# Block 1 of a three-block layer: convolution sums moved from SBUF to PSUM, compressed-attention operands split once

## The chip, the cores and the metric

The kernel runs on one core of a Trainium2 chip. The metric is the device time of one execution in microseconds (us). Five engines work side by side, each through its own queue in program order: TensorE (PE in the profile, its weight loads PEld), VectorE (DVE), ScalarE (ACT), GpSimd (POOL) and SyncE (SP), which here issues the DMAs. SBUF is the on-chip working memory; PSUM has 8 banks of 128 x 512 fp32, and PE writes its products there.

## The reference, cut to what matters

Three blocks follow each other over 512 tokens of 1024 features. The change lies in the first, which sums an attention branch with three parts and a convolution branch:

```python
def compress_blocks(t, pos_emb, w1, w2):            # 31 blocks of 32 tokens, for each of 4 groups
    ...
    return jax.nn.silu(blocks @ w1) @ w2

# in nsa_attention, for every block of 128 queries:
s_c = jnp.einsum('bgrqd,bgnd->bgrqn', qb, k_c).astype(jnp.float32) * scale
p_c = masked_softmax(s_c, c_end[None, :] <= tpos[:, None])
o_c = jnp.einsum('bgrqn,bgnd->bgrqd', p_c.astype(dt), v_c)
...
return gb[..., 0:1] * o_c + gb[..., 1:2] * o_s + gb[..., 2:3] * o_w

# in conformer_conv: 31 taps over time, each feature for itself, then a layer norm
z = u_a * jax.nn.sigmoid(u_b)
zp = jnp.pad(z, ((0, 0), (CONV_WIDTH - 1, 0), (0, 0)))
z = lax.conv_general_dilated(zp, conv_w, window_strides=(1,), padding='VALID', ...) + conv_b
```

With 512 tokens all 8 selection blocks are taken (top 16 of 8), so the selected branch `o_s` is a causal attention over all keys, like the window branch `o_w`.

## The kernel before

Features lie on partitions, tokens along the free axis; a matrix of 1024 features is eight tiles of 128x512. Nearly every product is made of three fp32r products: each operand is split into a high part and the rest (`h`, `l`), and `gemm` (L169 to L177) issues `h*h`, `l*h`, `h*l` for each of 8 steps, so 24 matmuls of 512 columns into one PSUM bank. Weights come by DMA into `wst` and are split by ACT (`wh`, L158) and POOL (`wl`, L159).

Block 1 up to the norm behind the convolution is one stage in which everything runs at once:

- **Convolution** (`conv_gate`, `conv_in`, `conv_taps`, L652 to L682). For each of eight feature tiles `c` two products give `z`, 128 x (30 + 512) in SBUF. `conv_taps` starts the sum `y = X[:, c]` with tap 0 on ACT (L672), then 30 taps on DVE (L682), each reading `z` shifted, the tap's weight (one per partition) and `y`, and writing `y`. All taps have low priority (`LOW` = 3000), so they stand where DVE would otherwise have nothing to do. `X` holds eight tiles, so several sums can be open at once.
- **Compressed branch.** `compress` makes the 31 compressed keys and values of four groups, `done_k` and `done_v` leave them in `kcT` and `vcs` (fp32). For each group `compressed(g, qs)` (L875 to L922) splits its keys into two zero-padded operands `KCz` with 16 small ACT and DVE instructions (L880 to L883), makes the scores, the softmax and the transposed probabilities `pcT`, and splits the values (L917 to L921). `mix_compressed` (L966 to L972) splits the probabilities of 128 queries, one head at a time, into two zero-padded operands `PCz` (ACT L969, DVE L970) and multiplies them, as the first products of the output bank `O`.
- **Selected and window branches.** `scores` (L924) and `mix` (L953) for each group `g`, 4 query blocks and 2 branches: scores to PSUM, maximum on DVE (L938), exponential on ACT (L939), scaling on ACT or POOL, transposes on PE (L957), split by ACT (L960) and DVE (L961), products (L963, L964).
- Between them stand projections and gates by a list of letters (`ORD`).

The order of instructions on each engine comes from a scheduler that lays them out ahead of the run by its own costs and the priorities; on the chip each engine takes its queue in that order.

PSUM in this stage: three banks for products (`g`), two for scores, two for transposes, one for `O`:

```python
K.psum(g=3, s=2, pt=2, o=1)
...
y = X[:, c]
nc.scalar.activation(y, z[:, 0:T], AF.Identity, scale=w(0), bias=K.v("conv_b", c))
for k in range(30, n, -1):          # n is 0 here
    nc.vector.scalar_tensor_tensor(y, z[:, k:k + T], w(k), y, op0=MUL, op1=ADD)
...
for h in range(4):                  # mix_compressed
    r = slice(h * 32, (h + 1) * 32)
    nc.scalar.activation(PCz[0][r, h], pcT[r, i * P:(i + 1) * P], AF.Copy)
    nc.vector.tensor_tensor(PCz[1][r, h], pcT[r, i * P:(i + 1) * P], PCz[0][r, h], SUB)
```

Behind the stage the `Norm` (L250 on) subtracts a shift from each tile of `X` (L309), sums the tiles and their squares (L280), takes column sums on PE (L201), makes mean and inverse deviation (L324 to L227), and the normed tiles become the operands `zn` of the next product with `w_conv_out`. Beside this PE makes eight more projections (`sgc`, evicted by L688).

Of the kernel before, what the change touches and what calls it, by code (L numbers as in the profile page):

```python
# [19 lines left out]
P = 128  # L20
# [26 lines left out]
TAP = ""  # L47
TC0, TC1 = 4,8
TPB = 1
# [20 lines left out]
class Ker:  # L70
# [133 lines left out]
    def rstd(self, ps, scale, eps, out, sl=slice(0, T), back=True):  # L204
        """(scale * ps + eps)^-1/2: from the logarithm, and a step of Newton's."""
# [8 lines left out]
    def newton(self, v, out, t, meanwhile=None, back=True):  # L214
        """out <- v^-1/2; v and t are lost."""
# [34 lines left out]
class Norm:  # L250
    """Layer norm over the eight [P, T] tiles of X, in place, without gain and bias.

    A tile is fed as soon as it is there. The mean of the first two shifts all of them, so that one
    pass gives the variance. With a gain and a bias [P, 8], the first products behind the norm start
    ahead of its statistics, on the shifted tiles times the gain: r * (product - mu * W'gain) + W'bias."""
# [26 lines left out]
    def square(self, k, s):  # L282
        """s: squares that belong to the variance."""
# [57 lines left out]
    def head(self, units):  # L341
        """Products of the first units (weights, outputs each) with the norm's result, all but the last steps of each."""
# [37 lines left out]
class Vecs:  # L380
    """Per-feature vectors, one column for 128 features each."""
# [28 lines left out]
def _pos_cols(a):  # L410
    # [32, 64] -> [128 = (copy, d), e * 16 + kt] of value a[2 kt + e, d]
# [25 lines left out]
def _dm(w):  # L437
    """[K, M] -> [M/128, 128, K]: the stationary tiles of one block of 128 outputs side by side."""
# [5 lines left out]
def _group(a, n):  # L444
    """[U, 128, C] -> [U/n, 128, n*C]: n units side by side."""
# [4 lines left out]
def _dmk(w, cuts):  # L450
    """As _dm, with K cut in parts: part after part, flat."""
# [8 lines left out]
def _tm(w, per):  # L460
    """[K, M] -> [K/128/per, 128, per*M]: moving tiles, per k tiles in a unit."""
# [132 lines left out]
def block1(K, X, entry):  # L594
    """X: the residual tile [P, 8, T]; takes the input from DRAM, leaves the output before the last norm."""
# [3 lines left out]
    K.psum(g=3, s=2, pt=2, o=1)  # L599
# [7 lines left out]
    # operands g * x and the rms of x, applied behind the products  # L607
# [60 lines left out]
    def conv_taps(c, z):  # L668
        y = X[:, c]
        w = lambda k: K.v("conv_w", c * 31 + k)  # L670
        with tc.high_priority(offset=-LOW):
            nc.scalar.activation(y, z[:, 0:T], AF.Identity, scale=w(0), bias=K.v("conv_b", c))  # L672
            n = len(TAP) if TC0 <= c < TC1 else 0
            for k in range(n):
                t = pz.tile([P, T], F32, tag="tb", bufs=TPB, name=K.nm("tb"))
                if TAP[k] == "A":
                    nc.scalar.activation(t, z[:, k + 1:k + 1 + T], AF.Copy, scale=w(k + 1))
                else:
                    nc.gpsimd.tensor_tensor(t, z[:, k + 1:k + 1 + T], w(k + 1).to_broadcast([P, T]), MUL)
                nc.gpsimd.tensor_tensor(y, y, t, ADD)  # L680
# [22 lines left out]
    def roped(w, scale=1.0, out=None):  # L703
        """A projection times the rms factor, rotated: its sine and cosine have the factor."""
# [15 lines left out]
    def gates():  # L720
        # gates of the three branches, tokens on partitions
# [12 lines left out]
    # compressed keys and values  # L734
    def compress(pB, kv, src, done):
        """src: two [P, T] tiles of (group, d) rows; by quarters; done gets the transposed hidden layer and w2."""
# [37 lines left out]
        hT = pB.tile([P, 256], F32, tag="hT", name=K.nm("hT"))  # L774
        nc.vector.tensor_scalar(hT, pt[:, :256], 0.5, None, op0=MUL)
        w2 = pB.tile([P, 128], F32, tag="w2", name=K.nm("w2"))
        nc.sync.dma_start(w2, I[f"cw2_{kv}"][0])
# [46 lines left out]
    # static zero-padded operands of the compressed branch  # L824
    KCz = []
    PCz = []
    for i in range(2):
        t = pA.tile([P, 4, P], F32R, name=f"KCz{i}")
        nc.gpsimd.memset(t.bitcast(F32), 0.0)
        KCz.append(t)  # L830
        t = pA.tile([P, 4, P], F32R, name=f"PCz{i}")
# [3 lines left out]
    def values(pair):  # L835
        """Values of two groups, tokens on partitions: [tok, j, branch, (h | l)] each."""
# [38 lines left out]
    def compressed(g, qs):  # L875
        """Scores of the four heads over the compressed keys, softmax, transposed back: probabilities and values."""
        src = kcT[:, g * 32:(g + 1) * 32]
        for h in range(4):
            c = slice(h * 32, (h + 1) * 32)
            nc.scalar.activation(KCz[0][0:64, h, c], src, AF.Copy)  # L880
            nc.scalar.activation(KCz[0][64:128, h, c], src, AF.Copy)
            nc.vector.tensor_tensor(KCz[1][0:64, h, c], src, KCz[0][0:64, h, c], SUB)
            nc.vector.tensor_tensor(KCz[1][64:128, h, c], src, KCz[0][0:64, h, c], SUB)  # L883
        ps = K.ps("pt")
        for h in range(4):
            for e in range(2):
                nc.tensor.matmul(ps, lhsT=KCz[e][:, h], rhs=qs[h], start=h == 0 and e == 0, stop=h == 3 and e == 1)
        sT = pT.tile([P, T], F32, tag="ct", bufs=2, name=K.nm("ct"))
# [4 lines left out]
        sc = pT.tile([P, T], F32, tag="ct", bufs=2, name=K.nm("ct"))  # L893
# [1193 lines left out]
```

## Time and profile before

| | |
|---|---|
| Median of three runs | 2956.25 us (2956.14 to 2957.11) |
| Span of the profiled execution | 2957.2 us |
| First tap starts, last tap starts (of the 240) | 77.4 us, 583.7 us |
| First product of `w_conv_out` starts | 620.8 us |
| Busy over the whole span | PE 91%, DVE 62%, POOL 45%, ACT 44% |

No other time is given for the profiled execution than its span, which is 0.95 us above the median. "Busy" counts the time in which an engine has an instruction in work; for PE the ends are modelled, so a busy PE need not run at its peak. Mean durations are those of one instruction; where the next one of an in-order engine overlaps its end, the next one starts earlier than the duration says. PEclk is the granted share of TensorE's clock. A stretch is a piece of the span between two times; here the stretches are cut at the first tap (77.4), at the four times when a group's compressed scores reach DVE (222.3, 307.8, 393.9, 476.8), at the last tap (583.7) and at the first product behind the norm (620.8).

### The profile page before, as it was taken

To read this page: it belongs to the slowest core of one execution; us is meant where nothing else is said; L and a number is where in the kernel's file an instruction comes from. 1 tells how busy PE (TensorE), PEld (TensorE's weight loads), DVE (VectorE), ACT (ScalarE), POOL (GpSimd) and SP (SyncE) were. 2 spreads that over 40 slices of the span, in tenths; PEclk is the share of its full clock that TensorE was granted. 3 is DMA by queue.
4 is the path that set the end of the run, shared out by engine and by line. 5 is a ranking of instruction groups with operands and counts; after the bars stand their busy time and mean duration, and the time that the engine had idled before them with its cause. 6 is when DMAs were issued, how large, how long until landed. Compare 5 with 4: busy or idle time off the path is not lost.

```text
span 2957.2 us, 34250 instructions
## 1 busy us (share of the span) xinstructions
PE 2701.9 (91%) x12194; PEld 2137.6 (72%) x12194; DVE 1847.5 (62%) x2893; ACT 1295.3 (44%) x2396; POOL 1336.8 (45%) x1023
## 2 busy tenths in 40 slices
PE   7778998899999998888889999999989889999997
PEld 5556766677888875666667778887766668788885
DVE  7999999986342477676675831115877865422246
ACT  3337786443222254354344433332556652322233
POOL 6564343444444454333332544444555334444442
PEclk9889999999999999999999999999999899999998
DMA  3221111132232322322321222223232122222223
GB/s 113 93 80 45 45 39 50 51 107 93 93 100 93 100 73 79 87 65 62 90 65 59 79 90 96 94 97 110 82 104 72 50 72 93 93 93 94 99 93 100
DMA packets 78666, 243.26 MB, mean 82 GB/s; under 512 B 10528, under 2 KB 14793, under 8 KB 78497
## 3 DMA queue, kind: packets, MB, share of 16 engines
q1 hardware_dynamic: 78496, 241.09, 25.3%
q8 instruction: 96, 1.57, 0.2%
q14 instruction: 74, 0.60, 0.1%
HBM read 230.90 MB, written 4.52 MB: 80 GB/s over the span
## 4 chain that ended last, share of the span: by engine, by line
PE 59%; DVE 22%; ACT 5%; DMA 3%; issue 2%; POOL 1%; DVEq 0%; ACTq 0%; SPq 0%; POOLq 0%
PE pg L174 17%; PE pg L175 17%; PE pg L176 17%; DVE X L682 2%; DMA B<-diag 2%; DVE p L1896 1%; DVE QK L1312 1%; DMA diag<-dg 1%; DVE X L339 1%; PE ppt L957 1%; DVE PTl L961 1%; DVE ln L280 1%; PE ps L935 1%; DVE s L938 1%; DVE Zt L1418 1%
## 5 line engine op out<-in xcount | busy, mean ns | idle before, releaser
L159 POOL TENSOR_TENSOR wl<-wst,wh 128x512 fp32r<-128x512 f32 (+1 forms) x808 | 1111.2, 1381 | 1347.5 <-ACT wh L158 1260.3
L158 ACT ACTIVATE wh<-wst 128x512 fp32r<-128x512 f32 (+1 forms) x808 | 500.3, 627 | 1106.8 <-PE pg L175 918.5
L174 PE MATMUL pg<-op,wh 128*128 128x512 f32 (+1 forms) x2008 | 813.2, 405 | 12.8 <-ACT wh L158 6.7
L176 PE MATMUL pg<-op,wl 128*128 128x512 f32 (+1 forms) x2008 | 809.9, 403 | 10.0 <-POOL wl L159 10.0
L175 PE MATMUL pg<-op,wh 128*128 128x512 f32 (+1 forms) x2008 | 807.2, 402 | 1.4 <-DVE op L194 1.4
L174 PEld LDWEIGHTS pg<-op,wh 128*128 128x128 f32 (+1 forms) x2008 | 387.5, 193 | 92.9 <-ACT wh L158 7.3
L176 PEld LDWEIGHTS pg<-op,wl 128*128 128x128 f32 (+1 forms) x2008 | 387.0, 193 | 91.9 <-POOL wl L159 13.5
L175 PEld LDWEIGHTS pg<-op,wh 128*128 128x128 f32 (+1 forms) x2008 | 387.3, 193 | 80.7 <-DVE op L194 3.9
L174 PE MATMUL pg<-hid,wh 128*128 128x512 f32 x688 | 272.2, 396 | 0.8 <-DVE hid L193 0.8
L175 PE MATMUL pg<-hid,wh 128*128 128x512 f32 x688 | 271.8, 395 | 1.3 <-DVE hid L194 1.3
L176 PE MATMUL pg<-hid,wl 128*128 128x512 f32 x688 | 272.1, 396 | 0.0
L682 DVE SCALAR_TENSOR_TENSOR X<-z,vec,X 128x512 f32<-128x512 f32 x240 | 233.6, 1006 | 1.3
L1122 DVE TENSOR_TENSOR X<-X,pg 128x512 f32<-128x512 f32 x56 | 38.6, 689 | 222.4 <-PE pg L176 222.4
L175 PEld LDWEIGHTS pg<-hid,wh 128*128 128x128 f32 x688 | 129.2, 188 | 33.0 <-DVE hid L194 1.6
L174 PEld LDWEIGHTS pg<-hid,wh 128*128 128x128 f32 x688 | 129.2, 188 | 32.8 <-DVE hid L193 1.3
L176 PEld LDWEIGHTS pg<-hid,wl 128*128 128x128 f32 x688 | 129.2, 188 | 31.5 <-issue 0.2
L193 DVE CAST hid<-t 128x512 fp32r<-128x512 f32 x86 | 52.2, 607 | 147.1 <-ACT t L1099 146.3
L939 ACT ACTIVATE P<-ps,s 128x128 f32<-128x128 f32 (+3 forms) x128 | 66.3, 522 | 20.6 <-DVE s L938 17.3
L1113 DVE SCALAR_TENSOR_TENSOR t<-pg,R 128x512 f32<-128x512 f32 x32 | 22.1, 692 | 84.0 <-PE pg L176 83.9
L194 DVE TENSOR_TENSOR hid<-t,hid 128x512 fp32r<-128x512 f32 x86 | 64.7, 752 | 3.0
L938 DVE TENSOR_REDUCE s<-ps 128x1 f32<-128x128 f32 (+3 forms) x128 | 59.4, 481 | 7.7 <-PE ps L937 6.7
L935 PE MATMUL ps<-sk,sk 128*128 128x256 f32 (+2 forms) x128 | 48.8, 382 | 8.2 <-ACT P L939 7.6
(524 smaller groups left out, 4445.8 us busy)
## 6 DMA issues: line engine op xcount, KB each, us to landing
wst<-in_w_f_dram SPq DMA_DIRECT2D x64, 512.0 KB
wst<-in_w_up_dram SPq DMA_DIRECT2D x32, 512.0 KB
wst<-in_w_down_dram SPq DMA_DIRECT2D x32, 512.0 KB
wst<-in_w_ga_dram SPq DMA_DIRECT2D x24, 512.0 KB
wst<-in_w_fg_dram SPq DMA_DIRECT2D x22, 512.0 KB
wst<-in_w_fu_dram SPq DMA_DIRECT2D x22, 512.0 KB
wst<-in_w_q_dram SPq DMA_DIRECT2D x16, 512.0 KB
wst<-in_w_out_dram SPq DMA_DIRECT2D x16, 512.0 KB
```

Source lines behind the costliest of these rows:

```text
L158: nc.scalar.activation(h, st, AF.Copy)
L159: nc.gpsimd.tensor_tensor(l, st, h, SUB)
L174: self.nc.tensor.matmul(ps, lhsT=wh, rhs=h[:, sl], start=first and k == 0, stop=False)
L175: self.nc.tensor.matmul(ps, lhsT=wh, rhs=l[:, sl], start=False, stop=False)
L176: self.nc.tensor.matmul(ps, lhsT=wl, rhs=h[:, sl], start=False, stop=last and k == n - 1)
L193: nc.vector.tensor_copy(h, src)
L194: nc.vector.tensor_tensor(l, src, h, SUB)
L682: nc.vector.scalar_tensor_tensor(y, z[:, k:k + T], w(k), y, op0=MUL, op1=ADD)
L935: nc.tensor.matmul(S[:, :N], lhsT=ql, rhs=kh[:, :N], start=True, stop=False)
L938: nc.vector.tensor_reduce(mx[:, h:h + 1], S[:, :L], AX, MAX, negate=True)
L939: nc.scalar.activation(Pt[h][:, :L], S[:, :L], AF.Exp, bias=mx[:, h:h + 1], accum_out=den[:, h:h + 1])
L1122: nc.vector.tensor_tensor(X[:, m], X[:, m], ps, ADD)
```

## The change

Five things change, all in block 1:

1. The sum of a convolution tile is held in a PSUM bank `y`, of which there is one; ACT starts it there with tap 0, DVE adds 30 taps in place, and ACT copies the end to `X[:, c]`. One product bank is given up for it (`g=2`).
2. `done_k` splits the compressed keys of all groups at once (`KC`), on 128 partitions; for each group two ACT copies with a broadcast put four heads of them into `KCz`, which is 640 wide, so that one instruction reaches all four diagonal blocks.
3. `done_v` splits the values of all groups at once (`VC`, four copies of a group's 32 rows by a wider `hT`).
4. The transposed probabilities are split straight from PSUM into `PCz`, for two query blocks at a time (`pad_compressed`): 8 ACT and 8 DVE instructions a group where there were 16 and 16.
5. The compressed products are the last of an output bank instead of the first.

Dead code of the taps goes (`TAP` is the empty string), and comments; the lines are renumbered by two or three.

```diff
-    K.psum(g=3, s=2, pt=2, o=1)
+    K.psum(g=2, s=2, pt=2, o=1, y=1)
...
-    kcT = pA.tile([64, P], F32, name="kcT")
-    vcs = pA.tile([P, 64], F32, name="vcs")
+    KC = [pA.tile([P, P], F32R, name=f"KC{e}") for e in range(2)]
+    VC = pA.tile([P, 4, P], F32R, name="VC")
...
     def conv_taps(c, z):
-        y = X[:, c]
         w = lambda k: K.v("conv_w", c * 31 + k)
         with tc.high_priority(offset=-LOW):
+            y = K.ps("y")
             nc.scalar.activation(y, z[:, 0:T], AF.Identity, scale=w(0), bias=K.v("conv_b", c))
...
-            for k in range(30, n, -1):
+            for k in range(30, 0, -1):
                 nc.vector.scalar_tensor_tensor(y, z[:, k:k + T], w(k), y, op0=MUL, op1=ADD)
+            nc.scalar.activation(X[:, c], y, AF.Copy)
...
-        hT = pB.tile([P, 256], F32, tag="hT", name=K.nm("hT"))
-        nc.vector.tensor_scalar(hT, pt[:, :256], 0.5, None, op0=MUL)
...
+        n = 1 if kv == "k" else 4
+        hT = pB.tile([P, 8, n, 32], F32, tag=f"hT{kv}", name=K.nm("hT"))
+        nc.vector.tensor_scalar(hT, pt[:, :256].rearrange("p (a n) -> p a n", n=32)[:, :, None, :].to_broadcast([P, 8, n, 32]), 0.5, None, op0=MUL)
...
+        nc.scalar.activation(KC[0], ps[:, :P], AF.Copy)
+        nc.vector.tensor_tensor(KC[1], ps[:, :P], KC[0], SUB)
...
+        nc.scalar.activation(VC[:, :, 0:64], src, AF.Copy)
+        nc.vector.tensor_tensor(VC[:, :, 64:128], src, VC[:, :, 0:64], SUB)
...
     def compressed(g, qs):
-        src = kcT[:, g * 32:(g + 1) * 32]
-        for h in range(4):
-            c = slice(h * 32, (h + 1) * 32)
-            nc.scalar.activation(KCz[0][0:64, h, c], src, AF.Copy)
-            nc.scalar.activation(KCz[0][64:128, h, c], src, AF.Copy)
-            nc.vector.tensor_tensor(KCz[1][0:64, h, c], src, KCz[0][0:64, h, c], SUB)
-            nc.vector.tensor_tensor(KCz[1][64:128, h, c], src, KCz[0][0:64, h, c], SUB)
+        for e in range(2):
+            src = KC[e][:, g * 32:(g + 1) * 32][:, None, :].to_broadcast([P, 4, 32])
+            nc.scalar.activation(KCz[e].rearrange("p (h c) -> p h c", h=4)[:, :, 0:32], src, AF.Copy)
...
+        return sc
+
+    def pad_compressed(sc, half):
         ps = K.ps("pt")
-        for i in range(4):
-            nc.tensor.transpose(ps[:, i * P:(i + 1) * P], sc[:, i * P:(i + 1) * P], K.ident)
-        pcT = pT.tile([P, T], F32, tag="pcT", bufs=1, name=K.nm("pcT"))
-        nc.scalar.activation(pcT, ps, AF.Copy)
...
+        for a in range(2):
+            i = 2 * half + a
+            nc.tensor.transpose(ps[:, a * P:(a + 1) * P], sc[:, i * P:(i + 1) * P], K.ident)
         for h in range(4):
-            nc.scalar.activation(VC[h * 32:(h + 1) * 32, 64:128], vl[gs], AF.Copy)
-        return pcT, VC
+            r = slice(h * 32, (h + 1) * 32)
+            src = ps[r, :256].rearrange("p (a q) -> p a q", a=2)
+            nc.scalar.activation(PCz[0][r, :, h], src, AF.Copy)
+            nc.vector.tensor_tensor(PCz[1][r, :, h], src, PCz[0][r, :, h], SUB)
...
-                mix_compressed(O, i, pcT, VC)
-            mix(O, g, i, b, Pt, VS[g // 2][g % 2], False, b == 1)
+            mix(O, g, i, b, Pt, VS[g // 2][g % 2], b == 0, False)
             if b == 1:
+                mix_compressed(O, g, i)
+                if i == 1:
+                    pad_compressed(sc, 1)
```

Beside the code, the order on the engines moves. Three places matter. The first is VectorE in the first stretch. Names ending in a number are buffers: `z_472` and `z_581` are the inputs of the tiles 0 and 1 of the convolution, `X` holds all sums. Before:

```order
L682 SCALAR_TENSOR_TENSOR X<-z_472,vec,X 128x512
L682 SCALAR_TENSOR_TENSOR X<-z_581,vec,X 128x512
L655 TENSOR_TENSOR zb_739<-pg_704,R_43_242 128x512
L682 SCALAR_TENSOR_TENSOR X<-z_472,vec,X 128x512
L682 SCALAR_TENSOR_TENSOR X<-z_581,vec,X 128x512
```

The same place in the change, where `z_473` and `z_584` are the inputs of tiles 0 and 1, and `py_476` is the bank with the sum of tile 0:

```order
L673 SCALAR_TENSOR_TENSOR py_476<-z_473,vec,py_476 128x512 x6
L660 SCALAR_TENSOR_TENSOR t_582<-pg_547,R_43_242 128x512
L673 SCALAR_TENSOR_TENSOR py_476<-z_473,vec,py_476 128x512
L663 SCALAR_TENSOR_TENSOR z_584<-zb_544,t_582 128x512
L673 SCALAR_TENSOR_TENSOR py_476<-z_473,vec,py_476 128x512 x11
L653 TENSOR_TENSOR zb_744<-pg_709,R_43_242 128x512
L673 SCALAR_TENSOR_TENSOR py_476<-z_473,vec,py_476 128x512 x4
```

Before, taps of two sums stood in turn. Now one sum runs at a time: 130 of the 240 taps stand directly behind a tap of their own sum, where 23 did.

The second place is VectorE at the end of the convolution. Before (`X<-X,c` shifts a tile for the norm, `ln` are its sums, `mu` its mean):

```order
L682 SCALAR_TENSOR_TENSOR X<-z_4682,vec,X 128x512 x4
L688 TENSOR_TENSOR t_5549<-pg_5514,R_43_242 128x512
L682 SCALAR_TENSOR_TENSOR X<-z_4682,vec,X 128x512 x6
L688 TENSOR_TENSOR t_5588<-pg_5553,R_43_242 128x512
L682 SCALAR_TENSOR_TENSOR X<-z_4682,vec,X 128x512 x2
L309 TENSOR_TENSOR X<-X,c_5368 128x512
L280 TENSOR_TENSOR ln_5364<-ln_5364,X 128x512
L280 TENSOR_TENSOR ln_5372<-ln_5372,ln_5404 128x512
L324 TENSOR_SCALAR mu_5412<-pm_5408 128x512
```

In the change, from the end of tile 6 (`py_3670`) and all of tile 7 (`py_4552`) on:

```order
L673 SCALAR_TENSOR_TENSOR py_3670<-z_3667,vec,py_3670 128x512 x4
L673 SCALAR_TENSOR_TENSOR py_4552<-z_4549,vec,py_4552 128x512 x30
L296 SCALAR_TENSOR_TENSOR ln_5222<-c_5226,ln_5222 128x512
L306 TENSOR_TENSOR X<-X,c_5226 128x512 x4
L277 TENSOR_TENSOR ln_5230<-ln_5230,ln_5233 128x512
L277 TENSOR_TENSOR ln_5222<-ln_5222,X 128x512
```

The 30 taps of the last tile now stand in one block behind the attention's last instructions, and all of the norm's shifts and sums behind them. Between the last tap and `mu` stood 3 instructions and stand 23.

The third place is ScalarE in the norm, from the square of the mean to the inverse deviation (`r`), with the loads of its tables of functions (`gc` is the hyperbolic tangent of a projection, `ln` and `r` logarithm and exponential). Before:

```order
L326 ACTIVATE ln_5415<-mu_5412 128x512
L212 ACT_TABLE_LOAD
L158 ACTIVATE wh_5677<-wst_5671 128x512
L219 ACTIVATE ln_5415<-ln_5417 128x512
L220 ACTIVATE r_5413<-ln_5415 128x512
L212 ACT_TABLE_LOAD
```

In the change:

```order
L323 ACTIVATE ln_5273<-mu_5270 128x512
L209 ACT_TABLE_LOAD
L1015 ACT_TABLE_LOAD
L1015 ACTIVATE gc_5332<-t_5368 128x512
L216 ACT_TABLE_LOAD
L216 ACTIVATE ln_5273<-ln_5275 128x512
L155 ACTIVATE wh_5453<-wst_5451 128x512
L217 ACT_TABLE_LOAD
L217 ACTIVATE r_5271<-ln_5273 128x512
```

A tangent with its table now stands inside, and the program has three table loads more (77, and 74 before). From within the products with `w_conv_out` on, all engines have their instructions in the same order as before.

## Rows read from the trace of the kernel before

**Rows 1.** Page, busy tenths of PE and DVE in 40 slices of the span

```profile
PE   7778998899999998888889999999989889999997
DVE  7999999986342477676675831115877865422246
```

**Rows 2.** Windows by stretch: time, busy PE, PEld, DVE, ACT, POOL (instructions), PEclk, DMA

```profile
77.40:222.30 144.90, 108.50 (x493) 85.94 (x493) 135.85 (x166) 46.65 (x100) 90.52 (x55) 0.83 0.27 86
222.30:307.80 85.50, 75.98 (x388) 57.28 (x387) 79.20 (x160) 68.11 (x185) 36.11 (x30) 0.96 0.11 37
307.80:393.90 86.10, 77.72 (x435) 61.02 (x434) 81.64 (x159) 62.17 (x161) 36.49 (x31) 0.98 0.15 46
393.90:476.80 82.90, 74.68 (x375) 55.73 (x374) 80.02 (x147) 61.44 (x154) 35.64 (x29) 0.98 0.17 51
476.80:583.70 106.90, 96.38 (x473) 73.52 (x472) 103.56 (x177) 65.60 (x160) 38.71 (x28) 0.99 0.15 52
583.70:620.80 37.10, 30.22 (x99) 20.33 (x99) 35.39 (x43) 22.04 (x35) 19.64 (x13) 0.78 0.26 86
750.00:800.00 50.00, 50.00 (x219) 40.88 (x218) 17.34 (x23) 13.05 (x23) 23.46 (x21) 1.00 0.28 85
```

**Rows 3.** Groups by form, DVE, 0 to 660 us: count, busy us, mean ns, idle

```profile
L682 DVE SCALAR_TENSOR_TENSOR X<-z,vec,X 128x512 f32<-128x512 f32 x240 | 233.6, 1006 | 1.3
L961 DVE TENSOR_TENSOR PTl<-ppt,PTh 128x512 fp32r<-128x512 f32 x80 | 52.8, 682 | 3.0 <-ACT PTh L960 2.5
L970 DVE TENSOR_TENSOR PCz<-pcT,PCz 32x128 fp32r<-32x128 f32 x64 | 27.7, 432 | 1.1
...
L688 DVE TENSOR_TENSOR t<-pg,R 128x512 f32<-128x512 f32 x16 | 10.9, 680 | 0.0
...
L883 DVE TENSOR_TENSOR KCz<-kcT,KCz 64x32 fp32r<-64x32 f32 x16 | 6.3, 393 | 0.3
...
L882 DVE TENSOR_TENSOR KCz<-kcT,KCz 64x32 fp32r<-64x32 f32 x16 | 5.1, 318 | 0.2
...
L770 DVE SCALAR_TENSOR_TENSOR t<-t,pg 128x256 f32<-128x256 f32 x2 | 0.8, 406 | 0.0
```

**Rows 4.** The tile X on DVE: shortest, median, longest of one tap in ns

```profile
L682 DVE SCALAR_TENSOR_TENSOR X<-z,vec,X x240: 714/746/1878, 77.4 to 583.7; 128x512 f32<-128x512 f32 x120
```

**Rows 5.** Timelines of DVE and of POOL at 547 us: start, us

```profile
546.70 2.45 DVE L682 SCALAR_TENSOR_TENSOR X<-z,vec,X 128x512 f32<-128x512 f32 x2
...
547.05 1.54 POOL L159 TENSOR_TENSOR wl<-wst,wh 128x512 fp32r<-128x512 f32 x1 [6.38 <-ACT wh L158]
```

**Rows 6.** Timeline of DVE: two taps of different sums, merged

```profile
113.12 1.40 DVE L682 SCALAR_TENSOR_TENSOR X<-z,vec,X 128x512 f32<-128x512 f32 x2
```

**Rows 7.** Chain that ended last: start, us, two taps of one sum

```profile
580.05 0.76 DVE X L682
580.84 0.76 DVE X L682
```

**Rows 8.** Groups, PE, 222.3 to 476.8 us: count, busy us, mean ns, idle and releaser

```profile
L174 PE MATMUL pg<-op,wh 128*128 128x512 f32 x126 | 53.7, 426 | 0.0
...
L957 PE MATMUL ppt<-ident,P 128*128 128x128 f32 x240 | 40.8, 287 | 2.4 <-POOL P L950 2.1
L964 PE MATMUL po<-PTl,VS 128*128 128x512 f32 x60 | 26.2, 436 | 11.3 <-DVE PTl L961 11.3
```

**Rows 9.** Groups, ACT, 0 to 660 us: count, busy us, mean ns, idle

```profile
L672 ACT ACTIVATE X<-z,vec 128x512 f32<-128x512 f32 x8 | 6.5, 812 | 33.3 <-DVE z L665 33.3
...
L212 ACT ACT_TABLE_LOAD x4 | 5.1, 1283 | 0.1
...
L913 ACT ACTIVATE pcT<-ppt 128x512 f32<-128x512 f32 x4 | 2.4, 595 | 9.5 <-PE ppt L911 9.5
```

**Rows 10.** Chain that ended last, from the norm's mean on: start, us

```profile
585.93 2.09 PE pm L201 x2
...
620.78 1.22 PE pg L174 x2
```

More of the change, by code (lines that the diff above doesn't have):

```diff
@@ L46 @@
 GA = 2
-TAP = ""
-TC0, TC1 = 4,8
-TPB = 1
 EV = (4,4,5)
@@ L668, in conv_taps @@
     def conv_taps(c, z):
-        y = X[:, c]
         w = lambda k: K.v("conv_w", c * 31 + k)
         with tc.high_priority(offset=-LOW):
+            y = K.ps("y")
             nc.scalar.activation(y, z[:, 0:T], AF.Identity, scale=w(0), bias=K.v("conv_b", c))
[L673 to L680, printed above, removed]
-            for k in range(30, n, -1):
+            for k in range(30, 0, -1):
                 nc.vector.scalar_tensor_tensor(y, z[:, k:k + T], w(k), y, op0=MUL, op1=ADD)
+            nc.scalar.activation(X[:, c], y, AF.Copy)
     def proj(w, scale=None, out=None):
@@ L773, in compress @@
             nc.tensor.transpose(pt[:, j * P:(j + 1) * P], hsl[:, j * P:(j + 1) * P], K.ident)
-        hT = pB.tile([P, 256], F32, tag="hT", name=K.nm("hT"))
-        nc.vector.tensor_scalar(hT, pt[:, :256], 0.5, None, op0=MUL)
-        w2 = pB.tile([P, 128], F32, tag="w2", name=K.nm("w2"))
-        nc.sync.dma_start(w2, I[f"cw2_{kv}"][0])
+        n = 1 if kv == "k" else 4
+        hT = pB.tile([P, 8, n, 32], F32, tag=f"hT{kv}", name=K.nm("hT"))
+        nc.vector.tensor_scalar(hT, pt[:, :256].rearrange("p (a n) -> p a n", n=32)[:, :, None, :].to_broadcast([P, 8, n, 32]), 0.5, None, op0=MUL)
+        hT = hT.rearrange("p a h n -> p (a h n)")
+        w2 = pB.tile([P, 2, 2, 64], F32, tag="w2", name=K.nm("w2"))
+        for e in range(2 if kv == "k" else 1):
+            nc.sync.dma_start(w2[:, :, e], I[f"cw2_{kv}"][0].rearrange("p (j d) -> p j d", j=2))
         done(hT, w2)
@@ L783, in done_k @@
         for j in range(2):
-            nc.tensor.matmul(ps[:64, :P], lhsT=w2[:, j * 64:(j + 1) * 64], rhs=hT[:, j * P:(j + 1) * P], start=j == 0, stop=j == 1)
-        nc.vector.tensor_copy(kcT, ps[:64, :P])
+            nc.tensor.matmul(ps[:, :P], lhsT=w2[:, j].rearrange("p c d -> p (c d)"), rhs=hT[:, j * P:(j + 1) * P], start=j == 0, stop=j == 1)
+        nc.scalar.activation(KC[0], ps[:, :P], AF.Copy)
+        nc.vector.tensor_tensor(KC[1], ps[:, :P], KC[0], SUB)
     def done_v(hT, w2):
         ps = K.ps("pt")
-        for j in range(2):
-            nc.tensor.matmul(ps[:, :64], lhsT=hT[:, j * P:(j + 1) * P], rhs=w2[:, j * 64:(j + 1) * 64], start=j == 0, stop=j == 1)
-        nc.vector.tensor_copy(vcs, ps[:, :64])
+        for g in range(4):
+            for j in range(2):
+                h = hT[:, (4 * j + g) * P:(4 * j + g + 1) * P]
+                nc.tensor.matmul(ps[:, g * 64:(g + 1) * 64], lhsT=h, rhs=w2[:, j, 0], start=j == 0, stop=j == 1)
+        src = ps[:, :256].rearrange("p (g d) -> p g d", g=4)
+        nc.scalar.activation(VC[:, :, 0:64], src, AF.Copy)
+        nc.vector.tensor_tensor(VC[:, :, 64:128], src, VC[:, :, 0:64], SUB)
     def seq(fs):
@@ L825, in block1 @@
     KCz = []
+    for i in range(2):
+        t = pA.tile([P, 640], F32R, name=f"KCz{i}")
+        nc.gpsimd.memset(t.bitcast(F32), 0.0)
+        KCz.append(t)
     PCz = []
     for i in range(2):
[L828 to L831, printed above, removed]
+        t = pA.tile([P, 2, 4, P], F32R, name=f"PCz{i}")
         nc.gpsimd.memset(t.bitcast(F32), 0.0)
@@ L886, in compressed @@
             for e in range(2):
-                nc.tensor.matmul(ps, lhsT=KCz[e][:, h], rhs=qs[h], start=h == 0 and e == 0, stop=h == 3 and e == 1)
-        sT = pT.tile([P, T], F32, tag="ct", bufs=2, name=K.nm("ct"))
+                nc.tensor.matmul(ps, lhsT=KCz[e][:, h * P:(h + 1) * P], rhs=qs[h], start=h == 0 and e == 0, stop=h == 3 and e == 1)
+        sT = K.tmp()
         nc.scalar.activation(sT, ps, AF.Copy)
@@ L892, in compressed @@
             nc.tensor.transpose(ps[:, i * P:(i + 1) * P], sT[:, i * P:(i + 1) * P], K.ident)
-        sc = pT.tile([P, T], F32, tag="ct", bufs=2, name=K.nm("ct"))
+        sc = pT.tile([P, T], F32, tag="ct", bufs=1, name=K.nm("ct"))
         four = lambda t: t.rearrange("p (i h n) -> p i h n", i=4, h=4)
@@ L964, in mix, with mix_compressed @@
             nc.tensor.matmul(O, lhsT=V, rhs=tl, start=False, stop=last and j == i)
-    def mix_compressed(O, i, pcT, VC):
-        for h in range(4):
-            r = slice(h * 32, (h + 1) * 32)
-            nc.scalar.activation(PCz[0][r, h], pcT[r, i * P:(i + 1) * P], AF.Copy)
-            nc.vector.tensor_tensor(PCz[1][r, h], pcT[r, i * P:(i + 1) * P], PCz[0][r, h], SUB)
+    def mix_compressed(O, g, i):
         for e in range(2):
-            nc.tensor.matmul(O, lhsT=VC, rhs=PCz[e].rearrange("p h q -> p (h q)"), start=e == 0, stop=False)
+            nc.tensor.matmul(O, lhsT=VC[:, g], rhs=PCz[e][:, i % 2].rearrange("p h q -> p (h q)"), start=False, stop=e == 1)
     todo["q"] = seq([f for g in range(4) for f in keys_queries(g)])
@@ L981, in block1 @@
         fill = list(ORD[2 + g])
-        pcT, VC = compressed(g, qs)
+        sc = compressed(g, qs)
+        pad_compressed(sc, 0)
         steps = [(i, b) for i in range(4) for b in range(2)]
```

6 lines of the change are left out of this document (removed).

## The prediction, made before the changed kernel was run

> **What bounds the kernel now.** I read the page's slices first. PE is at seven to nine tenths in every slice and DVE at nine only in the first seven and a half, some 560 us [rows 1]. So I cut that piece into stretches [rows 2]. From the first tap to the last (506.3 us) DVE is busy for 135.9 + 79.2 + 81.6 + 80.0 + 103.6 = 480.3 us, 95%, while PE loses time: its idle time before the products with the split probabilities ends on DVE, 11.3 us in three stretches [rows 8]. DVE sets the end of this piece. Behind it comes the norm, 37.1 us from the last tap to the next product at 620.8 us [rows 2, 10]; behind that, PE bounds the rest and the order does not change, so what is won or lost by 620.8 us goes into the total one for one.
>
> Where does DVE's time go? The taps are nearly half of it: 233.6 us for 240 [rows 3]. Their mean is 1006 ns, but their median only 746 and their longest 1878 [rows 4]. The timelines show what makes the slow ones: two taps took 2.45 us while POOL was in a weight split of 1.54 us [rows 5]. Both read two tensors from SBUF. The instructions of the same width with one input in PSUM do not show it: 680 and 682 ns on average over 16 and 80 [rows 3].
>
> **The change part by part, as VectorE's work.**
>
> *The slow taps.* With the sum in PSUM, a tap reads one tensor from SBUF. I take it to run like the undisturbed ones now, 746 ns: 240 x (1006 - 746) = -62.4 us [rows 3, 4]. No row has DVE writing to PSUM, so the price of that is unknown. From below it is bounded by the 680 ns of an instruction that reads PSUM without a weight per partition, another -16 us; from above by the 1006 ns of now, which would take back all 62. I stay at 746, since the nearest rows show no difference between reading PSUM (682) and SBUF.
>
> [...]
>
> *One sum at a time.* Two taps of different sums took 1.40 us, so the second started 0.66 us after the first [rows 6]; two of one sum start 0.79 us apart [rows 7]. Of the taps 130 now stand behind their own sum instead of 23, 107 x 0.12 = +12.8 us.
>
> *Operands of the compressed branch.* The probabilities cost 64 x 432 ns = 27.7 us; now 32 instructions of 256 elements with an input in PSUM, 406 ns by the nearest row, 13.0 us: -14.7. The keys' 6.3 + 5.1 us become one instruction of 128x128 (under 0.41): -11.0 [rows 3]. The values' few small ones and the wider `hT` I set at nothing together; each is below 1.5 us, and either sign lies inside the rounding.
>
> Sum for DVE: -62.4 + 12.8 - 14.7 - 11.0 = -75.3 us.
>
> *What ACT gets.* Fewer and larger instructions, eight copies of 0.60 us more [rows 9]. It is busy for 61 to 68 us of the 83 to 86 in a group's stretch [rows 2], so this costs nothing as long as no one waits for a particular one. Someone does at each change of tile: the bank is free when ACT has copied it (0.60) and begun the next sum (0.81) [rows 9], some 1.5 us with the handing over. By the new order four of the seven changes have five or more other instructions of DVE between the sums, three have none or one: 3 x 1.5 = +4.5 us. From below nothing, if the tap behind is not late; from above 7 x 1.5.
>
> *The norm.* It still begins in order behind the last taps, but with 20 more instructions between the last tap and the mean. They are moved, not added, and stand in DVE's sum already. New in series are ACT's copy and the shift it makes behind it, 2 x 0.6, a first square of 0.6, and three table loads of 1.28 [rows 9]: +5.7, say 6. PE makes more of its eight projections behind the mean instead of under the taps: 135 matmuls of 0.228 us (50 us over 219, [rows 2]) are 31 us, and the mean to the next product took 35 us before (585.9 to 620.8, [rows 10]). [...]
>
> *What is late next: PE.* In the three middle stretches (254.5 us) I count PE's matmuls in the program by their columns, 0.228 us for 512: 378 of projections (126 groups of three, [rows 8]), 216 others of 512, 48 of 384, 193 of 256, 264 transposes of 128 columns (240 of them in [rows 8]) and 96 small ones, about 196 us. DVE has 240.9 there now; of the 75 some 45 fall here, so 196 too. Two engines that hand work to each other in a fixed order cannot both be full. DVE now idles 13.6 us of these 254.5 [rows 2]; I take 31, so that both are at 86%: +18 us. From below 0; from above 35, the products' share of time in which PE stands now.
>
> **Total:** -75.3 + 4.5 + 6 + 18 = -47 us. The profiled span is 2957.2 us, so 2910; against the median, 0.95 lower, 2956.25 - 47 = 2909.
>
> **The rivals.**
>
> *Everything full.* The waits do not grow (0 for 18, 1 for 4.5) and the taps take nearer 700 ns (-8): -76, 2880 us. For it: DVE was 97% busy beside PE at 90% in the fourth and fifth stretch. Against: PE has as much to do as DVE there now.
>
> *Two banks are too few.* The compress products hold one bank over other projections in the first stretch, and DVE's order there has up to 11 taps in a row (11 x 0.79 = 8.7 us) between two evictions, when a projection lasts 24 x 0.228 = 5.5 us. Then PE waits up to 3 us at some ten projections and comes late to everything: +25, 2934 us. Against: PE stood idle there anyway, 36 of 145 us [rows 2].
>
> *Nothing gained in the taps.* The weight per partition comes from SBUF as well; if POOL's splits held the tap up by that, 1006 ns would stay: -47 + 62 = +15, 2971 us. Against: it would be a second reader of one word only.
>
> *One bank, read and written by the same instruction.* The slower side, one mechanism at one place: no row has an engine reading and writing the same PSUM bank element by element. If the two passes took turns, a tap would cost one more pass of 512, twice what 256 more elements cost (680 - 406 = 274 ns), 0.55 us: 240 x 0.55 = 132, total +85, 3041 us. It decides from a tap of 746 + 47000/240 = 942 ns on. Against it: PE adds to a bank at 0.228 us for 512 columns, a read and a write each.
>
> **How the numbers follow.** The forecast (-30 to -63) has 0.48, everything full 0.20, two banks too few (-6 to -30) 0.16, nothing gained in the taps 0.05, the bank read and written in turn 0.05; 0.06 is for a result within 0.2% (5.9 us, about what a measurement can tell from no change). So faster 0.84, same 0.06, slower 0.10. The range from 2872 (the full case with taps somewhat cheaper yet) to 2944 leaves out the last part of the two-bank case, the same and the slower ones, about 0.18, and little below.
>
> **What would show it.** Right: taps in `py` at 700 to 800 ns with no long ones; DVE's busy share in the middle stretches near 86%, these 76 us long each; the last tap near 515 us, the first product of `w_conv_out` 57 to 60 us behind it; the rest of the span as before. Wrong: taps above 940 ns; a middle stretch still at 83 us with DVE below 80%, its idle time ended by PE or by ACT's copies; PE idle before projections with their releaser in DVE's evictions.

## The result

The changed kernel takes 2909.84 us, the median of four runs (2904.16 to 2911.59), beside 2956.68 for the kernel before (2956.14 to 2957.11): a ratio of 0.9843, with a 95% interval of 0.9828 to 0.9859. That is 46.8 us less; 47 were forecast. Measured again later it was 2906.5 us and 0.9825 (0.981 to 0.9839).

The windows of the changed kernel, cut at the events of [rows 2] as far as the last tap (first tap, a group's compressed scores four times, last tap), with a last one up to where the last operand of the norm is ready; then its DVE groups for 0 to 660 us and the taps as a tile. The columns are those of before.

```profile
77.40:185.90 108.50, 96.30 (x511) 78.73 (x512) 94.58 (x139) 42.76 (x79) 66.79 (x54) 0.98 0.32 103
185.90:261.70 75.80, 74.44 (x398) 56.55 (x397) 69.79 (x139) 62.49 (x162) 34.27 (x32) 1.00 0.18 59
261.70:339.00 77.30, 73.87 (x432) 58.78 (x432) 69.57 (x143) 59.06 (x147) 32.97 (x30) 1.00 0.17 51
339.00:415.20 76.20, 72.08 (x371) 54.42 (x370) 68.38 (x129) 58.19 (x137) 33.67 (x30) 1.00 0.18 54
415.20:518.00 102.80, 85.47 (x414) 63.20 (x412) 93.70 (x168) 56.61 (x139) 21.06 (x20) 0.92 0.10 35
518.00:578.00 60.00, 45.47 (x166) 34.29 (x167) 56.16 (x72) 36.73 (x57) 35.27 (x19) 0.79 0.28 86
```

```profile
L673 DVE SCALAR_TENSOR_TENSOR py<-z,vec,py 128x512 f32<-128x512 f32 x240 | 180.2, 751 | 10.9 <-ACT py L671 6.2
...
L921 DVE TENSOR_TENSOR PCz<-ppt,PCz 32x256 fp32r<-32x256 f32 x32 | 13.4, 419 | 2.2 <-ACT PCz L920 1.3
...
L941 DVE TENSOR_TENSOR s<-s,GT 128x4 f32<-128x4 f32 x32 | 11.4, 356 | 0.1
...
L663 DVE SCALAR_TENSOR_TENSOR z<-zb,t 128x512 f32<-128x512 f32 x8 | 9.8, 1220 | 0.0
...
L336 DVE TENSOR_TENSOR X<-X,r 128x512 f32<-128x512 f32 x8 | 9.4, 1220 | 0.0
...
L194 DVE SCALAR_TENSOR_TENSOR zn<-X,zn 128x512 fp32r<-128x512 f32 x8 | 7.5, 939 | 0.0
```

```profile
L673 DVE SCALAR_TENSOR_TENSOR py<-z,vec,py x240: 718/756/757, 77.4 to 518.0; 128x512 f32<-128x512 f32 x120
```

Read the last row against [rows 4]: no tap takes longer than 757 ns, where the longest took 1878. The last tap starts at 518.0 instead of 583.7 us. The stretches went from 144.9, 85.5, 86.1, 82.9 and 106.9 us [rows 2] to 108.5, 75.8, 77.3, 76.2 and 102.8. Only the norm behind the last tap got longer.

Where the piece ends for TensorE shows best in its products with the norm's operands `zn` (tile view; first and last start). First the row of before, then that of the change:

```profile
L174 PE MATMUL pg<-zn,wh x64: 390/394/796, 608.2 to 663.3; 128*128 128x512 f32 x64
```

```profile
L171 PE MATMUL pg<-zn,wh x64: 392/396/398, 573.9 to 618.3; 128*128 128x512 f32 x64
```

The last of them starts 45.0 us earlier. I use this number, the last start of that row, as the marker of block 1 in all that follows; it leaves out what the rest of the program adds. From there to the end the order is the same, and the profiled execution of the change, the fastest of its four (2904.16 us), gains some 10 us more there, which no run explains; the other three, at 2908.5 to 2911.6, lie within 4 us of what the marker gives.

The row of before also corrects an event that the table of before and the prediction use. The first product with `zn` started at 608.2 us; the one at 620.8 us belongs to the sixth of the first output's eight steps. The last `zn` was split from 625.6 us on and ready at 626.3, so that is the time to set beside the end of the last window above.

One new stall stands out. In TensorE's list of waits from 415 to 580 us (what waited, for whom, us in total, times, longest) and in ScalarE's timeline at its end:

```profile
PE pg L171 <- ACT wh L155: 18.7, 1, 18.7
PE pm L198 <- DVE ln L277: 6.7, 1, 6.7
```

```profile
518.81 0.60 ACT L674 ACTIVATE X<-py 128x512 f32<-128x512 f32 x1 [23.78 <-DVE py L673]
519.31 0.59 ACT L295 ACTIVATE c<-pm 128x512 f32<-128x512 f32 x1
```

ScalarE's queue has the copy of the last sum in front. It waits 23.8 us there for 30 taps in a row, and the weight splits `wh` behind it wait too, and TensorE with them. The experiments ask what that costs.

### The profile page after: what moved, and what is told of

The parts are those of the page before. It is cut to its first block, busy times and chain, and to the rows that moved or that the text cites. A ratio compares the mean times of both kernels' runs of the same rounds, so it can differ in the third digit from the quotient of the medians.

```text
span 2902.4 us, 34153 instructions
## 1 busy us (share of the span) xinstructions
PE 2676.3 (92%) x12206; PEld 2120.0 (73%) x12206; DVE 1780.9 (61%) x2825; ACT 1283.2 (44%) x2317; POOL 1306.6 (45%) x1023
## 4 chain that ended last, share of the span: by engine, by line
PE 63%; DVE 23%; ACT 6%; DMA 3%; issue 3%; POOL 2%; SPq 0%; DVEq 0%; ACTq 0%; POOLq 0%
PE pg L172 18%; PE pg L173 18%; PE pg L171 18%; DMA B<-diag 2%; DVE p L1894 1%; DVE py L673 1%; DVE X L336 1%; DVE QK L1310 1%; PE ppt L956 1%; POOL wl L156 1%; DMA diag<-dg 1%; DVE ln L277 1%; DVE Zt L1416 1%; PE ps L934 1%; DVE Z L1417 1%
## 5 line engine op out<-in xcount | busy, mean ns | idle before, releaser
L156 POOL TENSOR_TENSOR wl<-wst,wh 128x512 fp32r<-128x512 f32 (+1 forms) x808 | 1099.9, 1367 | 1367.1 <-ACT wh L155 1285.7
L673 DVE SCALAR_TENSOR_TENSOR py<-z,vec,py 128x512 f32<-128x512 f32 x240 | 180.2, 751 | 10.9 <-ACT py L671 6.2
L960 DVE TENSOR_TENSOR PTl<-ppt,PTh 128x512 fp32r<-128x512 f32 x80 | 53.4, 684 | 4.7 <-ACT PTh L959 3.9
```

The costliest lines, as they stand in the source:

```text
L156: nc.gpsimd.tensor_tensor(l, st, h, SUB)
L960: nc.vector.tensor_tensor(tl, pt, th, SUB)
```

## The experiments

### The two halves of the change, each alone

The first kernel is the one before with the new sums and banks:

```diff
-    K.psum(g=3, s=2, pt=2, o=1)
+    K.psum(g=2, s=2, pt=2, o=1, y=1)
...
-        y = X[:, c]
...
+            y = K.ps("y")
...
+            nc.scalar.activation(X[:, c], y, AF.Copy)
```

> The kernel before with the convolution's sums in a PSUM bank and two banks for products; the compressed branch as before. Theory (VectorE's work sets the end, and the taps were slow because they read two tensors from SBUF beside GpSimd's weight splits): taps at 750 ns with none over 800, 62 us of work less and 13 back for sums one at a time; by the share of VectorE's saving that the whole change turned into time (47 of 75) some 30 us less than before, about 2926 us. Rival (the shorter compressed branch carries the gain): within 10 us of before.

The second is the changed kernel with the sums back in SBUF (`y = X[:, c]`, no copy, `g=3`):

> The changed kernel with the sums back in SBUF and three banks for products, so only the compressed branch is changed. Theory: taps as slow as before (mean near 1000 ns), 26 us of VectorE's work less, by the same share some 16 us less than before, about 2940 us. Rival (the compressed branch carries the gain): 30 us less or more. Second rival (it only takes idle time): within 6 us of before.

Measured: 2929.81 us for the sums alone (ratio 0.9912, 0.9896 to 0.9928) and 2934.23 for the compressed branch alone (0.9928, 0.9909 to 0.9946). By the marker 22.6 and 18.9 us, together 41.5 of the 45.0. The products with `zn` and then the taps, in the tile views, each time of the one and of the other:

```profile
L174 PE MATMUL pg<-zn,wh x64: 390/393/404, 596.5 to 640.7; 128*128 128x512 f32 x64
```

```profile
L171 PE MATMUL pg<-zn,wh x64: 390/395/795, 588.1 to 644.4; 128*128 128x512 f32 x64
```

```profile
L675 DVE SCALAR_TENSOR_TENSOR py<-z,vec,py x240: 716/756/757, 76.7 to 540.5; 128x512 f32<-128x512 f32 x120
```

```profile
L672 DVE SCALAR_TENSOR_TENSOR X<-z,vec,X x240: 706/742/1862, 77.2 to 558.6; 128x512 f32<-128x512 f32 x120
```

Both halves gain, and they nearly add up. The sum in PSUM is what ends the slow taps. The compressed branch, whose 26 us of VectorE's work I had let count for 16, gave 22 of the total and 19 by the marker; the sums alone gave 27 where I said 30. Both rivals fall: neither half carries it alone.

### One bank for products less, alone

```diff
-    K.psum(g=3, s=2, pt=2, o=1)
+    K.psum(g=2, s=2, pt=2, o=1)
```

> The kernel before with two banks for products where it had three, nothing else. Theory (TensorE waits for VectorE in this stage anyway): 0 to 6 us more. Rival (two banks are too few, projections wait for their evictions): 25 us more.

Measured 2960.51 us against 2956.59, a ratio of 1.0015 (1.0004 to 1.0026); by the marker 7.5 us later. Its first stretch:

```profile
76.00:223.50 147.50, 107.90 (x500) 85.88 (x500) 140.87 (x173) 49.41 (x106) 82.72 (x55) 0.86 0.25 79
```

The bank's price is small, as expected: the first stretch, where the prediction saw the waits, is 2.6 us longer than before, and the whole 4 to 8 us, not 25. This run has the taps of before; the order of the change, with its long rows of taps, shows the same: in all its waits from 77.4 to 415 us TensorE's products wait 6.3 us for VectorE's evictions, 3.1 at the longest. The rival of the prediction, "two banks are too few", falls.

### What is it about SBUF that makes a tap slow?

Two kernels tell a read from a write. In the first, the tap writes to the bank and reads its second tensor from SBUF; in the second it reads the bank and writes to SBUF:

```diff
-  nc.vector.scalar_tensor_tensor(y, z[:, k:k + T], w(k), y, op0=MUL, op1=ADD)
+  nc.vector.scalar_tensor_tensor(y, z[:, k:k + T], w(k), X[:, c], op0=MUL, op1=ADD)
```

```diff
-  nc.vector.scalar_tensor_tensor(y, z[:, k:k + T], w(k), y, op0=MUL, op1=ADD)
+  nc.vector.scalar_tensor_tensor(X[:, c], z[:, k:k + T], w(k), y, op0=MUL, op1=ADD)
```

> The changed kernel with each tap reading its second tensor from SBUF and still writing to the PSUM bank; the taps do not add up, the sum of all but the last is left out. Theory (two tensors read from SBUF beside a GpSimd instruction are what is slow): taps with a mean near 1000 ns again, over 60 of 240 above 900, and the gain mostly gone, 2935 us or more. Rival (writing to SBUF is what is slow): taps at 750, none above 800, 2910 us or less. By the side: the taps do not wait for one another's result, so neighbours should start 0.66 us apart where they started 0.79.

> The changed kernel with each tap reading the PSUM bank, where ScalarE has put tap 0, and writing to SBUF; the taps do not add up, the sum of all but the last and the copy from PSUM are left out. Theory (reading two tensors from SBUF is what is slow): taps at 750 ns, none above 800, 2900 to 2912 us. Rival (writing to SBUF beside GpSimd is what is slow): mean near 1000, 2935 us or more.

Measured in one run each: 2953.35 us with the read from SBUF, 2906.71 us with the write to SBUF. The two tile rows, in this order:

```profile
L673 DVE SCALAR_TENSOR_TENSOR py<-z,vec,X x240: 718/760/1866, 78.3 to 561.3; 128x512 f32<-128x512 f32 x120
```

```profile
L673 DVE SCALAR_TENSOR_TENSOR X<-z,vec,py x240: 711/748/751, 77.2 to 515.1; 128x512 f32<-128x512 f32 x120
```

The second tensor read from SBUF brings the 1.87 us back, with a mean of 1003 ns and 74 of the 240 taps over 900. Where the result goes does not matter: the longest tap takes 1866 ns into the bank and 1878 into SBUF [rows 4] with both tensors from SBUF, 757 and 751 with the sum from the bank.

The traces also show the other party. In the kernel before, 77 of the 240 taps took over 800 ns, and during every one of them GpSimd had an instruction in work; of the 113 taps without such an overlap none took over 753. In the change 123 taps overlap with GpSimd's work, and none takes over 757. No run takes GpSimd's work away.

The second kernel also compares the two sources of the sum: read from PSUM, with the result written to SBUF, the tap's median is 748 ns, against 746 from SBUF [rows 4].

The remark by the side failed: neighbours stayed at 0.79 us although no tap needs the other's result (the taps of the first kernel were at work for 240.6 us, which is 240 times their mean, so none overlapped the next). I take it that each of them still waits for the last writer of its output; no run tests that.

### ScalarE's copy out of the way

```diff
-            nc.scalar.activation(X[:, c], y, AF.Copy)
+            (nc.vector.tensor_copy(X[:, c], y) if c == 7 else nc.scalar.activation(X[:, c], y, AF.Copy))
```

> The changed kernel with the copy of the last convolution tile from PSUM to SBUF on VectorE, where ScalarE stood 23.8 us waiting for it with the weight splits of the gate products behind it. Theory (VectorE sets the end of this piece): TensorE's idle 18.7 us before the gate products goes, the splits then run beside taps that do not mind them, and the norm's instructions with two SBUF inputs get their 0.8 us back from 1.2; 3 to 6 us less than the changed kernel, about 2905. Rival (TensorE's 18.7 us are on the path): 15 us less or more. Second rival (nothing but the copy counts): 0 to 1 us more.

Measured 2908.03 us, a ratio of 0.9843 (0.9824 to 0.9862): as the change. But the run tells nothing of the question, since the wait only got another name. In TensorE's waits:

```profile
PE pg L171 <- DVE X L306: 19.6, 1, 19.6
```

Behind the copy stood two squares of the norm, which wait for shifts that VectorE makes behind the same 30 taps. The splits were still behind them.

### Less for TensorE to do

If the 18.7 us mattered through TensorE being late, taking products from it must help:

```diff
-        nc.scalar.activation(sgc[m], proj(I["w1_gc"][m]), AF.Tanh, scale=0.5)
+        tg = K.tmp()
+        nc.vector.tensor_tensor(tg, K.gemm(K.gps(), gx[:1] if m > 1 else gx, K.wunit(I["w1_gc"][m])), R, MUL)
+        nc.scalar.activation(sgc[m], tg, AF.Tanh, scale=0.5)
```

> The changed kernel with one of eight steps in six of the eight gate products beside the norm (the gates behind `w1_gc`), so that TensorE has 126 matmuls, some 29 us, less to do behind the last taps; seven eighths of these six products are left out, their weights are still split and VectorE's and ScalarE's instructions stay. Theory (VectorE sets the end of this piece, TensorE's idle 18.7 us cost nothing): the last operand `zn` is ready when it was, 2 us either way, and the total is that of the changed kernel within 4 us. Rival (TensorE, late by its idle time, sets the end): 15 us less or more.

Measured 2911.18 us, 0.9846 (0.9821 to 0.9871): no gain in the total, where the rival had 15 us less. But the other half of the expectation failed: the last `zn` came later, not when it was.

```profile
L194 DVE SCALAR_TENSOR_TENSOR zn<-X,zn x8: 682/688/693, 569.3 to 590.8; 128x512 fp32r<-128x512 f32 x8
```

In the change it starts at 577.5. VectorE waited 8.9 us for ScalarE, ScalarE 9.0 for a weight buffer, and TensorE for a `wl` of GpSimd. VectorE's wait, and GpSimd's timeline:

```profile
DVE X L1026 <- ACT ln L1025: 8.9, 1, 8.9
```

```profile
570.43 11.38 POOL L156 TENSOR_TENSOR wl<-wst,wh 128x512 fp32r<-128x512 f32 x3 [6.44 <-ACT wh L155]
```

The row puts three splits together. Looked at singly, the first took 8.93 us and the other two 1.26 and 1.27; the three that the view has by themselves took 1.27, 1.29 and 1.30. When the first began, VectorE was in a run of `X` times `r`, the tile times its sigmoid and the `zn` splits, without a pause and at their short durations; this run ended at 578.2 us, and the split 1.1 us later, at 579.4. So here it was GpSimd's split that got longer, where before it was the taps. With that new wait, which can have used up what TensorE saved, the run decides neither for the theory nor for the rival, and doesn't say what the 18.7 us cost by themselves.

### The last tile's taps behind the norm's first part

Here the last tile's taps are begun only when the other seven tiles have been fed to the norm, so the order gets the norm's shifts and sums first and the gates' evictions between the taps:

```diff
-        z = pz.tile([P, 30 + T], F32, tag="z", name=K.nm("z"))
+        z = (ap_ if c == 7 else pz).tile([P, 30 + T], F32, tag="z", bufs=1 if c == 7 else 2, name=K.nm("z"))
...
-        conv_taps(c, z)
+        (last.append(z) if c == 7 else conv_taps(c, z))
...
-    K.psum(g=5, m=3)
+    K.psum(g=4, m=3, y=1)
...
     for k in range(NT):
+        if k == 7: conv_taps(7, last[0])
         norm.feed(k)
```

The changed kernel ran again as a yardstick on the same chip.

> The changed kernel again, as the yardstick for the run with the last tile behind the norm's first part: about 2909 us by every theory.

> The changed kernel with the taps of the last convolution tile begun after the norm's shifts and sums of the other seven tiles, so that they stand between the gates' evictions; its input gets a buffer of its own, the other inputs two instead of three; the sum's bank stays through the norm. ScalarE's copy of the last sum then has no weight splits or squares behind it that TensorE waits for. Theory (VectorE's work sets the end of this piece, TensorE's 18.7 us idle is mostly its consequence): VectorE has the same work; its pauses of some 4 us between the norm's sums go, and with the weight splits beside taps the norm's instructions with two SBUF inputs come back from 1.2 to 0.8 us, some 5 us: 8 us less than the changed kernel. Rival (TensorE's idle 18.7 + 6.7 us are on the path): 20 us less or more. Second rival (two input buffers hold the projections up): as the changed kernel or slower.

Measured 2889.67 us (ratio 0.9768, 0.9754 to 0.9782) against 2906.5 for the change: 16.8 us less, the best of the study, and between theory and rival. The products with `zn`, of the yardstick and of this kernel:

```profile
L171 PE MATMUL pg<-zn,wh x64: 390/393/404, 574.8 to 619.1; 128*128 128x512 f32 x64
```

```profile
L171 PE MATMUL pg<-zn,wh x64: 387/389/767, 553.8 to 600.4; 128*128 128x512 f32 x64
```

The marker moves by 18.7 us, and the views part it. VectorE first: from the first tap until the last `zn` is ready, the windows of the yardstick and of this kernel.

```profile
77.20:416.10 338.90, 317.97 (x1706) 249.75 (x1707) 302.26 (x548) 222.41 (x521) 167.78 (x144) 0.99 0.22 70
416.10:579.10 163.00, 131.19 (x581) 97.78 (x580) 150.06 (x240) 93.35 (x196) 56.52 (x39) 0.87 0.16 54
```

```profile
77.30:418.40 341.10, 322.02 (x1705) 251.28 (x1706) 299.48 (x555) 225.48 (x523) 167.13 (x144) 0.98 0.21 69
418.40:568.70 150.30, 131.22 (x612) 100.97 (x612) 141.66 (x234) 89.97 (x194) 57.01 (x42) 0.94 0.20 66
```

Together 501.9 became 491.4 us; VectorE's busy time went from 452.3 to 441.1, its idle time stayed at 50. The work that went is in groups that read two tensors from SBUF. In the change three of them took 9.8, 7.5 and 9.4 us; here:

```profile
L663 DVE SCALAR_TENSOR_TENSOR z<-zb,t 128x512 f32<-128x512 f32 x8 | 6.0, 751 | 0.0
...
L194 DVE SCALAR_TENSOR_TENSOR zn<-X,zn 128x512 fp32r<-128x512 f32 x8 | 5.5, 685 | 0.1
...
L336 DVE TENSOR_TENSOR X<-X,r 128x512 f32<-128x512 f32 x8 | 5.1, 685 | 0.0
```

These three and `X<-ln,X`, the tile times its sigmoid (7.5 to 5.8), make 11.8 us less; the last two rows run at 685 ns now, near the 678 that the `zn` splits of the change have in the median. The small ones `s<-s,GT` gave 1.9 more and the norm's sums took 2.5 back (5.8 and 5.2 to 6.9 and 6.6). So 10.5 us are VectorE's, from groups that had been lengthened; the pauses I had counted on gave nothing. The other 8.2 us I put down to TensorE, by its order: in the change it has gate products to do until 573.9 us and only then begins on the `zn`, of which the first was split from 561.7 on; here it takes them as they come, from 553.8 on. That is the share of the rival that was right.

> The kernel with the last tile's taps behind the norm's first part, with three buffers for the other inputs again (their room is taken from the probabilities, nine buffers for ten). Theory (the two buffers held the first stretch up by 2 to 3 us): 2 to 3 us less than with two, about 2887. Rival (nine buffers for probabilities are too few): 2 us more or worse.

Measured 2890.48 us (0.9775, 0.9754 to 0.9796): no difference that these intervals could show, by the marker 1.8 us later. By its windows the piece up to the fourth group was 7.2 us shorter and the rest gave it back, so that the last `zn` is ready at the same time to 0.2 us; VectorE was busy for 443.8 us of 491.6, where it was 441.1 of 491.4:

```profile
77.10:411.00 333.90, 318.08 (x1709) 250.01 (x1709) 297.71 (x548) 223.50 (x523) 166.62 (x143) 0.98 0.22 72
411.00:568.70 157.70, 132.50 (x603) 100.63 (x601) 146.07 (x239) 91.67 (x193) 62.15 (x42) 0.92 0.17 57
```

### Two sums at once

```diff
-    K.psum(g=2, s=2, pt=2, o=1, y=1)
+    K.psum(g=2, s=2, pt=1, o=1, y=2)
```

> The changed kernel with two banks for sums and one for transposes instead of two, so that two sums run in turn. Theory: taps of different sums start 0.67 us apart where those of one sum took 0.79, so the first stretch, where taps follow each other, gets some 5 us shorter; in the middle stretches each transpose now waits for the split of the one before, which costs more than that, 20 us or more over the changed kernel. Rival (one sum at a time was the main loss of the change): 10 us less than the changed kernel.

Measured 2973.22 us, 1.0057 (1.0035 to 1.0079), over 60 us more than the change. Its first two stretches, and the largest waits of VectorE in the three middle ones:

```profile
77.70:185.70 108.00, 97.01 (x510) 80.07 (x511) 96.39 (x149) 43.32 (x80) 66.14 (x55) 0.97 0.32 103
185.70:285.00 99.30, 86.41 (x435) 63.35 (x435) 88.03 (x178) 66.82 (x173) 35.41 (x34) 0.97 0.16 51
```

```profile
DVE PTl L960 <- ACT PTh L959: 24.1, 18, 2.4
DVE s L939 <- ACT P L938: 13.9, 16, 2.6
```

Two sums in turn do run closer: eight taps in 5.36 us, 0.66 apart. Yet the first stretch gets 0.5 us shorter, not 5 (VectorE was idle there for 13.9 of its 108.5 us in the change already), and the middle stretches take 19 to 24 us more each, with VectorE waiting for the splits of the transposes that now have a single bank. The second sum isn't worth that bank.

## Why the prediction was right

The total is right to a microsecond, and the mechanism is shown by the runs; the terms are right less exactly. VectorE's work fell by 7.5 us less than forecast and the waits grew by 8.8 us less; that these two cancel is luck.

*The slow taps.* Forecast 746 ns and -62.4 us; measured 751 and 240 x (751 - 1006) = -61.2.

*One sum at a time, and the changes of tile.* Forecast +12.8 (0.79 less 0.66 is 0.13 and not 0.12, so it should have been 13.9) and +4.5. With the idle time in front of them, the taps held VectorE 233.6 + 1.3 us before and 180.2 + 10.9 now, so -43.8 where -45.1 was the sum of the three terms; 6.2 of the 10.9 are four changes of tile, for which I had three.

*The compressed branch.* Forecast -14.7 and -11.0; the probabilities went from 27.7 to 13.4 us (-14.3), and the keys from 11.4 to one instruction of 0.28 (-11.1).

*What I left out.* VectorE's busy time from the first tap until the last `zn` is ready (77.4 to 626.3 us before, 77.4 to 578.2 now) fell from 520.14 to 452.38 us, by 67.8 and not by 75.3. The taps, probabilities and keys by themselves fell by 53.4 + 14.3 + 11.1 = 78.8; all other work together took some 10 us more, where I had nothing. The taps do "run like the undisturbed ones"; the step that failed is to take it that the disturbance vanishes with them. GpSimd's work meets other instructions instead, which still read two tensors from SBUF: it lay beside 7 of the 8 `z<-zb,t` and 6 of the 8 `X<-X,r`, where it had been 2 of each. Their groups of before, against those above:

```profile
L942 DVE TENSOR_TENSOR s<-s,GT 128x4 f32<-128x4 f32 x32 | 9.4, 295 | 0.1
...
L665 DVE SCALAR_TENSOR_TENSOR z<-zb,t 128x512 f32<-128x512 f32 x8 | 6.4, 800 | 0.0
...
L339 DVE TENSOR_TENSOR X<-X,r 128x512 f32<-128x512 f32 x8 | 6.1, 802 | 0.0
L197 DVE SCALAR_TENSOR_TENSOR zn<-X,zn 128x512 fp32r<-128x512 f32 x8 | 6.0, 749 | 0.0
```

These four alone cost 2.0 + 3.4 + 3.3 + 1.5 = 10.2 us more; the other groups of this piece went up or down by 1.4 us at most and nearly cancel.

*What is late next: PE.* Mis-sized the other way. With the norm and the changes of tile I had 28.5 us of new waiting; over the same two windows VectorE's idle time rose from 28.8 to 48.4 us, by 19.7. In the middle stretches it was 21.6 of 229.3, where I said 31, so VectorE was busy for 90 to 92% of them and not 86, and their work fell by 33 us and not by 45. Their length came out at 76 us each all the same. The count of TensorE's matmuls behind the 31 doesn't add up either: by columns its terms make 186 us and not 196, and TensorE was busy for 96% of these stretches. -67.8 + 19.7 = -48.1 at the last `zn`, and -45.0 at the marker: TensorE is 3.1 us later behind it than it was before.

*The norm.* The products with `zn` start 55.9 us behind the last tap, the last `zn` 59.5; forecast 57 to 60. That 55.9 comes so near is luck too. The forecast counted from the product at 620.8 us; the first one stood at 608.2, 24.5 us behind the last tap and 22.3 behind the norm's column sums (585.9). Against these 22.3 us TensorE's 31 us of gate products, which the forecast set beside 35, are 9 too long. In the change the products with `zn` start 39.0 us behind the column sums (534.9 to 573.9), some 12 us after the first `zn` began to be split (561.7), because the gates were in front of them; the kernel with the last tile late gets 8 us back from TensorE by its order. VectorE itself idled behind the last tap for 3.8 us where it was 2.7, of the 6 that I had added.

*The rivals.* "Everything full" falls with the 19.7 us of new waiting. A bank read and written by one instruction costs next to nothing: the taps' mean is 751 ns, and 743 where the result goes to SBUF. Two banks cost 4 to 8 us, not 25. The weight, a reader of one word, made no tap slow beside GpSimd's splits: none is over 757.

## What to carry to other kernels

Look at the longest instruction of a group and not at its mean: where a few take more than twice the median (here 1878 ns against 746), ask which other engine was at work, and move one of the two inputs to PSUM (757 at the longest). The loss is then not all gone: here `z<-zb,t`, with two tensors from SBUF, went from a mean of 800 to 1220 ns, and `zn<-X`, with one, still took up to 1521 where its median is 414. The 80 splits `PTl`, with one input in PSUM, took 693 at most, also the 42 beside GpSimd's work, so put the other engine's work beside instructions like these. And behind a chain of low priority on one engine, look at the in-order queue of the engine that takes its result: what stands behind that copy waits for the whole chain, here 23.8 us.

## What was not expected of the hardware

- GpSimd was once the one that got longer: a weight split took 8.93 us beside a dense run of VectorE, where others of that view took 1.26 to 1.30, and ended 1.1 us after that run.
- TensorE's mean granted clock in the first stretch rose from 0.83 [rows 2] to 0.98, when its idle time there fell from 36.4 to 12.2 us: 12.2 us less busy time, for 511 recorded products beside 493. It was 0.97 with two sums at once, and 0.86 with one bank for products less and the taps of before. No run separates the clock from the shorter waits.
- Taps with the same output started 0.79 us apart even where none reads the other's result; with different outputs 0.66 (eight in 5.36 us).
